# The transposes of the rotary queries behind the key projections instead of behind the query projections

## The chip, the core and the metric

The kernel runs on one of the eight cores of a Trainium2 chip. A core has a matrix engine (TensorE, PE in the profile; PEld is its loading of weights), a vector engine (VectorE, DVE), an activation engine (ScalarE, ACT), GpSimdE (POOL) and SyncE (SP), which here only issues DMAs. Matrix products go to PSUM, which has eight banks of 512 float32 columns per partition; VectorE and ScalarE read them from there into SBUF. The metric is the device time of one launch in microseconds.

## The reference

The reference is a trunk of two post-norm layers over 256 positions of width 2048, in float32. The first layer mixes positions with a gated MLP, the second with latent attention; each mixer is followed by a gated MLP with a causal convolution, and each of the four sub-layers ends in a layer norm of `ALPHA * x + sublayer(x)`. The change lies in the attention, which is, cut to what matters:

```python
def mla_mixer(x, w_in, q_norm_g, kv_norm_g, w_q_b, w_kv_b, w_out, cos, sin):
    h = x @ w_in                                  # 2048 -> 512 + 512 + 64
    c_q, c_kv, k_rope = split(h)
    q = (rms_norm(c_q) @ w_q_b)                   # 16 heads of 128 + 64
    q_nope, q_rope = split(q)
    q_rope, k_rope = apply_rope(q_rope), apply_rope(k_rope)
    kv = (rms_norm(c_kv) @ w_kv_b)                # 16 heads of 128 + 128
    k_nope, v = split(kv)
    s = (q_nope . k_nope + q_rope . k_rope) * SM_SCALE   # per head, masked by chunks of 64
    return softmax(s) @ v, then @ w_out
```

Each head's score is a sum of two products: one over 128 columns that are not rotated, one over 64 that are. The rotated key is shared by all heads.

## The kernel before

The kernel is one straight program; there is no loop on the chip. A layer above the instructions keeps the order in which the code issues them, engine by engine, and adds the waits. All weights come from HBM as tiles of 128 x 2048 float32 (1 MB), through one list in the order of use (`Feed`, lines 48 to 92). A tile of weights is loaded into `raw` (line 62, from SP's queue). ScalarE rounds it to a narrower format as `wh` (line 75), VectorE writes the rest `raw - wh` as `wl` (line 76), each in two halves of 1024 columns. A product is then the sum of three: high times high, low times high, high times low. `feed.next()` gives the next tile and issues the splits of the two after it and the loads of two more.

All large tiles share one pool of 22 slots of SBUF (`big`), so a load or a split may have to wait until the last reader of an earlier tile has left its slot. All PSUM tiles share the eight banks (`bank`, pool `ps`) in the same way: the first matmul into a new bank waits for the last reader of the tile that had the bank before.

The part around the change is straight-line code:

1. Rotary queries (lines 609 to 618): the product for the 64 rotated columns of all 16 heads into four banks `qr`, for two halves b of the positions and two halves f of the columns. Between its two chunks stand the transposes `ct` of the key latent and `krt` of the rotated key.
2. Rotation (lines 619 to 622): VectorE reads each of the four banks in four operations (lines 527 to 530) and finishes in two more (531, 532). The result, `qr` in SBUF, is rounded by ScalarE and its rest taken by VectorE into `qrs`, one tile for each half of the positions (lines 626, 627).
3. `qr_put(b, f)` (lines 630 to 635): four transposes of `qrs[b]` for heads 4f to 4f+3 into a bank `qrt`, and a ScalarE copy of the bank into `qrT`.
4. `heads` (lines 638 to 651): 48 matmuls into four banks for four heads; then, for each bank, a ScalarE copy (line 649) and a VectorE subtraction (line 650) that split the result into `qnT` or `knT`. It is called four times for the queries (`qn`, tiles qn0 to qn3) and four times for the keys (`kn`).
5. The values `vv` (lines 715 to 729), in two halves; the scores of the first two heads begin inside the second half (`attend_a`, line 663). `attend_a` reads `qnT`, `knT`, `qrT` and `krT`. Then come the other heads, four steps ahead of the output projection.

In the kernel before, two calls of `qr_put` stand behind each of the four query blocks: qn0 is followed by heads 0 to 7 of the first half of the positions, and so on.

Of the kernel before, what the change touches and what calls it, by code (L numbers as in the profile page):

```python
# [95 lines left out]
def trunk(ctx: ExitStack, tc: tile.TileContext, x, xT, gm_in, gm_wout, ffn_up, ffn_dn,  # L96
# [9 lines left out]
    def slot(shape, name, dt=F32):  # L106
        return big.tile(shape, dt, tag="big", name=name)

    def bank(name):
        return ps.tile([P, 512], F32, tag="bank", name=name)  # L110

    def mm(o, l, r, start, stop):
        nc.tensor.matmul(o, l, r, start=start, stop=stop, skip_group_check=True)  # L113
# [516 lines left out]
    def qr_put(b, f):  # L630
        t = bank(f"qrt{b}{f}")
        for j in range(4):
            nc.tensor.transpose(t[:, j * P : (j + 1) * P], qrs[b][:, 4 * f + j].rearrange("p n c -> p (n c)"), ident)
        h = 4 * (f % 2)
        nc.scalar.copy(qrT[f // 2][:, h : h + 4, b * P : (b + 1) * P], t.rearrange("p (j c) -> p j c", j=4))


    def heads(dst, src, i, tag):
        hi, lo = feed.next()
        acc = [bank(f"{tag}{i}_{f}") for f in range(4)]  # L640
        for k in range(4):
            t = src[0][:, k, :]
            for n, (x, w) in enumerate(((t[:, 0:S], hi), (t[:, S : 2 * S], hi), (t[:, 0:S], lo))):
                for f in range(4):
                    o = k * 512 + f * P
                    mm(acc[f][:, 0:S], w[:, o : o + P], x, k == 0 and n == 0, k == 3 and n == 2)
        t = slot([P, 4, 2 * S], f"{tag}T{i}", F32R)
        for f in range(4):
            nc.scalar.copy(t[:, f, 0:S], acc[f][:, 0:S])
            nc.vector.tensor_tensor(t[:, f, S : 2 * S], acc[f][:, 0:S], t[:, f, 0:S].bitcast(F32), ALU.subtract)  # L650
        dst.append(t)

    for i in range(4):
        heads(qT, cq, i, "qn")
        for j in range(2):
            qr_put(i // 2, 2 * (i % 2) + j)
    for i in range(4):
        heads(kT, ckv, i, "kn")

    oT = []  # L660
    probs = {}
# [207 lines left out]
```

## Time and profile before

| | |
|---|---|
| time, median of three runs | 2544.89 us (2543.96, 2544.89, 2544.93) |
| time of the profiled execution | 2543.96 us |
| its span, first to last instruction | 2542.2 us |
| TensorE busy | 2524.2 us (99%) |
| mean granted TensorE clock | 0.998 |
| VectorE busy, ScalarE busy | 1575.4 us, 1230.3 us |
| HBM read | 476.00 MB, 188 GB/s over the span |

The profile is one execution; its times are microseconds from the first instruction. A row of the view in order of time gives the start, the duration, the engine, the line, the operation with `out<-in` by the program's names without numbers, the shape and how many instructions were merged; in brackets stands the idle time of the engine before it and what ended it. A row of a view by stretches gives the busy time of each engine within the stretch and the clock that TensorE was granted, as a share of full speed. A row of the waits names who waited for whom, the total, the number of times and the longest. Ends of matmuls are modelled, so the starts are what the arguments go by.

### The profile page before, as it was taken

How to read it: one execution, taken by the hardware profiler on the slowest of the kernel's cores; microseconds unless marked ns; L12 is line 12 of the kernel's file. 1: busy time of each engine (PE TensorE's matmuls, PEld its weight loads, DVE VectorE, ACT ScalarE, POOL GpSimd, SP SyncE). 2: the span in 40 equal slices, each digit the busy share in tenths (PEclk: the TensorE clock that was granted, in tenths of full speed). 3: DMA queues.
4: the chain of work that ended last, by engine and by line, in shares of the span. 5: the costliest groups of instructions: out<-in, count | busy, mean ns of one | idle time of the engine just before them, and what ended most of it. 6: DMA issues, size and time to landing. Idle time of an engine off the chain costs nothing.

```text
span 2542.2 us, 32529 instructions
## 1 busy us (share of the span) xinstructions
PE 2524.2 (99%) x13203; PEld 2161.4 (85%) x13203; DVE 1575.4 (62%) x2286; ACT 1230.3 (48%) x1805; POOL 2.9 (0%) x17
## 2 busy tenths in 40 slices
PE   9999999999999999999999999999999999999998
PEld 7888888888888888888888888988888888888886
DVE  6444675675455767665775547656676576667554
ACT  6343444455443555554554443555365555546441
POOL 0000000000000000000000000000000000000000
PEclk9999999999999999999999999999999999999999
DMA  8445444456564545555565553334555455546552
GB/s 338 183 169 195 166 177 172 174 214 225 201 221 165 205 166 202 184 180 183 185 226 202 207 221 146 122 142 177 187 199 182 166 199 182 182 168 246 209 199 89
DMA packets 68838, 480.20 MB, mean 189 GB/s; under 512 B 7632, under 2 KB 8272, under 8 KB 11728
## 3 DMA queue, kind: packets, MB, share of 16 engines
q1 hardware_dynamic: 68688, 478.13, 51.5%
q8 instruction: 103, 1.69, 0.3%
q14 instruction: 47, 0.39, 0.0%
HBM read 476.00 MB, written 2.10 MB: 188 GB/s over the span
## 4 chain that ended last, share of the span: by engine, by line
PE 98%; DVE 1%; DMA 0%; ACT 0%; SPq 0%; issue 0%; DVEq 0%; ACTq 0%
PE up L113 36%; PE dn L113 18%; PE u L113 11%; PE wo L113 10%; PE v L113 10%; PE mo L113 3%; PE upf L113 2%; PE mkv L113 1%; PE kn L113 1%; PE mq L113 1%; PE vv L113 1%; PE s L113 1%; PE qn L113 1%; PE sc L113 1%; PE qr L113 0%; PE lnt L369 0%
## 5 line engine op out<-in xcount | busy, mean ns | idle before, releaser
L76 DVE TENSOR_TENSOR wl<-raw,wh 128x1024 fp32r<-128x1024 f32 (+2 forms) x886 | 1054.3, 1215 | 534.5 <-ACT wh L75 375.5
L75 ACT CAST wh<-raw 128x1024 fp32r<-128x1024 f32 (+2 forms) x886 | 891.4, 1045 | 558.1 <-DVE wl L76 219.3
L113 PE MATMUL up<-xhl,wh 128*128 128x512 f32 x2624 | 715.1, 393 | 0.0
L113 PEld LDWEIGHTS up<-xhl,wh 128*128 128x128 f32 x2624 | 447.8, 188 | 54.9
L113 PEld LDWEIGHTS up<-xhl,wl 128*128 128x128 f32 x2624 | 403.5, 188 | 59.4
L113 PE MATMUL up<-xhl,wl 128*128 128x256 f32 x2624 | 420.1, 281 | 0.0
L113 PE MATMUL wo<-wh,woa 128*128 128x512 f32 x768 | 236.8, 389 | 0.0
L113 PE MATMUL v<-wh,xhl 128*128 128x512 f32 x768 | 235.8, 391 | 0.2 <-ACT wh L75 0.2
L113 PE MATMUL u<-xhl,wh 128*128 128x512 f32 x768 | 217.3, 396 | 0.0
L113 PE MATMUL dn<-wh,dn0a 128*128 128x512 f32 x688 | 212.2, 389 | 0.0
L113 PE MATMUL dn<-wh,dn1a 128*128 128x512 f32 x688 | 211.9, 389 | 0.0
L113 PEld LDWEIGHTS v<-wh,xhl 128*128 128x128 f32 x768 | 144.6, 188 | 31.4 <-ACT wh L75 0.6
L113 PEld LDWEIGHTS wo<-wh,woa 128*128 128x128 f32 x768 | 144.0, 188 | 29.9
L113 PEld LDWEIGHTS dn<-wh,dn1a 128*128 128x128 f32 x688 | 129.1, 188 | 26.9
L113 PEld LDWEIGHTS dn<-wh,dn0a 128*128 128x128 f32 x688 | 129.0, 188 | 26.5
L113 PE MATMUL wo<-wl,woa 128*128 128x512 f32 x384 | 149.2, 389 | 0.0
L113 PEld LDWEIGHTS u<-xhl,wh 128*128 128x128 f32 x768 | 131.5, 189 | 19.2 <-issue 1.1
L113 PE MATMUL v<-wl,xhl 128*128 128x512 f32 x384 | 147.2, 389 | 0.0
L113 PEld LDWEIGHTS u<-xhl,wl 128*128 128x128 f32 x768 | 121.3, 189 | 15.9
L113 PE MATMUL dn<-wl,dn0a 128*128 128x512 f32 x344 | 133.8, 389 | 0.0
L113 PE MATMUL dn<-wl,dn1a 128*128 128x512 f32 x344 | 133.8, 389 | 0.0
L113 PE MATMUL u<-xhl,wl 128*128 128x256 f32 x768 | 130.8, 281 | 0.0
(208 smaller groups left out, 2119.3 us busy)
## 6 DMA issues: line engine op xcount, KB each, us to landing
raw<-in_ffn_up_dram SPq DMA_DIRECT2D x172, 1024.0 KB, 4.8
raw<-in_gm_in_dram SPq DMA_DIRECT2D x95, 1024.0 KB, 4.8
raw<-in_ffn_dn_dram SPq DMA_DIRECT2D x86, 1024.0 KB, 4.7
raw<-in_gm_wout_dram SPq DMA_DIRECT2D x48, 1024.0 KB, 4.8
raw<-in_ml_out_dram SPq DMA_DIRECT2D x16, 1024.0 KB, 4.8
raw<-in_ml_b_dram SPq DMA_DIRECT2D x14, 1024.0 KB, 4.8
raw<-in_ml_kv_dram SPq DMA_DIRECT2D x5, 864.0 KB, 4.6
lng<-in_ln_rows_dram SPq DMA_DIRECT2D x4, 1024.0 KB, 6.7
```

The lines of the kernel that those rows point to most:

```text
L75: self.nc.scalar.copy(hi[:, c], raw[:, c])
L76: self.nc.vector.tensor_tensor(lo[:, c], raw[:, c], hi[:, c].bitcast(F32), ALU.subtract)
L113: nc.tensor.matmul(o, l, r, start=start, stop=stop, skip_group_check=True)
```

## The change

The eight calls of `qr_put` move from the loop over the query blocks to the loop over the key blocks, two behind each. Their order changes too: behind block i come heads 4i to 4i+3 of both halves of the positions, where before all heads of the first half came first.

```diff
     for i in range(4):
         heads(qT, cq, i, "qn")
-        for j in range(2):
-            qr_put(i // 2, 2 * (i % 2) + j)
     for i in range(4):
         heads(kT, ckv, i, "kn")
+        for b in range(2):
+            qr_put(b, i)
```

On TensorE the 32 transposes, in four groups of eight, then stand behind kn0 to kn3. On ScalarE the eight copies of line 635 stand behind the copies of the same key blocks. VectorE's and SP's instructions keep their order; which slot and which bank each tile gets, and so what its first writer waits for, changes from qn1 on. `qrs` is held until the last key block.

## The prediction

> **What bounds the kernel now.** I read the page first, then TensorE's waits, then the region around the moved transposes in order of time, engine by engine.
>
> ```profile
> span 2542.2 us, 32529 instructions
> PE 2524.2 (99%) x13203; PEld 2161.4 (85%) x13203; DVE 1575.4 (62%) x2286; ACT 1230.3 (48%) x1805; POOL 2.9 (0%) x17
> PE 98%; DVE 1%; DMA 0%; ACT 0%; SPq 0%; issue 0%; DVEq 0%; ACTq 0%
> ```
>
> TensorE's waits (engine and line that waited, for whom: us in total, times, longest):
>
> ```profile
> PE qrt L633 <- DVE qrs L627: 3.2, 1, 3.2
> PE o L113 <- ACT pts L700: 2.4, 1, 2.4
> ```
>
> TensorE is busy for 99% of the span and is 98% of the chain that ended last. So an edit that keeps its instructions can win only where it stands still or runs slowly. The largest wait of the whole run is at the first transposes of the rotary queries (qrt, line 633): 3.2 us until VectorE has written qrs. The edit moves exactly these transposes. TensorE in order of time (start, duration, instructions, and in brackets the idle time before them):
>
> ```profile
> 1608.31 1.12 PE L113 MATMUL qn<-cq,wh 128*128 128x256 f32 x8
> ...
> 1609.75 1.12 PE L113 MATMUL qn<-cq,wh 128*128 128x256 f32 x8
> ...
> 1612.15 0.64 PE L113 MATMUL qn<-cq,wl 128*128 128x256 f32 x4
> 1615.97 1.97 PE L633 MATMUL qrt<-ident,qrs 128*128 128x128 f32 x8 [3.19 <-DVE qrs L627]
> ...
> 1625.38 1.03 PE L633 MATMUL qrt<-ident,qrs 128*128 128x128 f32 x8
> 1626.17 1.19 PE L113 MATMUL qn<-cq,wh 128*128 128x256 f32 x8
> ...
> 1632.00 1.04 PE L633 MATMUL qrt<-ident,qrs 128*128 128x128 f32 x8
> ```
>
> Twelve matmuls go from 1608.31 to 1609.75, so one slot is 0.12 us and the 48 of a block of four heads take 5.76. The undisturbed round of eight transposes and 48 matmuls runs from 1625.38 to 1632.00: 6.62. The first round is different. The last four matmuls of qn0 start at 1612.15, so the next slot was free at 1612.63. From there to the end of that round is 1625.38 - 1612.63 = 12.75. The round therefore costs 12.75 - 6.62 = 6.13 more than an undisturbed one. The wait explains 1615.97 - 1612.63 = 3.34 of it. The other 2.79 is slowness after the wait, as the granted clock shows (columns: stretch, its length, then the busy time of PE, PEld, DVE, ACT and POOL, the clock as a share of full speed, DMA share, GB/s):
>
> ```profile
> 1611.60:1615.00 3.40, 1.19 (x10) 0.98 (x9) 3.40 (x11) 0.40 (x2) 0.00 (x0) 1.00 0.00 0
> 1615.00:1618.40 3.40, 2.43 (x12) 2.43 (x13) 3.37 (x4) 3.40 (x6) 0.00 (x0) 0.50 0.00 0
> 1618.40:1621.80 3.40, 3.40 (x17) 3.31 (x17) 3.32 (x6) 3.37 (x6) 0.00 (x0) 0.50 0.37 82
> 1622.00:1622.50 0.50, 0.50 (x6) 0.50 (x5) 0.50 (x2) 0.00 (x0) 0.00 (x0) 1.00 1.12 475
> ...
> 1686.60:1690.10 3.50, 2.41 (x20) 2.05 (x18) 3.06 (x5) 1.03 (x3) 0.00 (x0) 1.00 0.54 166
> 1690.10:1693.50 3.40, 2.08 (x16) 1.99 (x17) 1.14 (x4) 2.77 (x8) 0.00 (x0) 1.00 0.36 142
> ```
>
> The clock fell to 0.50 during the wait and came back only near 1621.8, inside qn1. The other long wait, 2.4 us near 1690 (o on pts), kept the clock at 1.00. So what the edit can win here is the 6.13, half of it hidden in matmuls that only look busy.
>
> **The change part by part.** It removes nothing and adds nothing: 32 transposes and eight ScalarE copies (line 635) move from behind qn0 to qn3, eight and two each, to behind kn0 to kn3.
>
> *The wait goes.* Behind qn0 now comes qn1, which does not read qrs. Behind kn0, some 25 us later, qrs has long been written. That gives back 6.13. It is the whole sum unless something else is late for qn1 or qn2, so I look at what is late next.
>
> *First new wait, qn1.* Each block takes four of the eight PSUM banks. In the changed program qn1 takes those of ct and qr, the fourth of them from qr of rows b=1, columns f=1. That bank is free when the rotation of that piece has read it for the last time, in line 530. VectorE in order of time:
>
> ```profile
> 1613.70 0.41 DVE L530 TENSOR_TENSOR qr<-qr,rope_sb 128x256 f32<-128x256 f32 x1
> ...
> 1614.70 2.48 DVE L627 TENSOR_TENSOR qrs<-qr,qrs 128x1024 f32<-128x1024 f32 x2
> 1617.09 2.35 DVE L76 TENSOR_TENSOR wl<-raw,wh 128x1024 fp32r<-128x1024 f32 x2
> 1619.36 1.41 DVE L650 TENSOR_TENSOR qnT<-qn,qnT 128x256 fp32r<-128x256 f32 x4
> 1620.86 2.36 DVE L76 TENSOR_TENSOR wl<-raw,wh 128x1024 fp32r<-128x1024 f32 x2
> ```
>
> Nothing on VectorE ahead of 1614 depends on what TensorE does after qn0, so this time stays: 1613.70 + 0.41 = 1614.11. TensorE started 0.05 behind the first qrs (1614.70 + 1.22 = 1615.92, then 1615.97), so I add that: 1614.16. It would have reached the fourth matmul of qn1 at 1612.63 + 3 x 0.12 = 1612.99. Wait: 1.17. Queued behind it on TensorE is everything, so it counts in full.
>
> *Second new wait, qn2.* Its four banks are those of qn0, free when line 650 has subtracted from them. VectorE's row stays where it is, since it stands behind qrs and a weight split, neither of which moves: its fourth piece ends at 1619.36 + 1.41 = 1620.77, with the 0.05 at 1620.82. TensorE would be at the fourth matmul of qn2 at 1614.16 + 48 x 0.12 = 1619.92. Wait: 0.90. It can't be less unless VectorE gets there sooner. In the kernel before, both waits lie inside the 6.13.
>
> *Third block and on.* VectorE then splits weights to 1623.22 and drains qn1 in four pieces of some 0.35, to about 1624.6. TensorE needs those banks from 1620.82 + 45 x 0.12 = 1626.22: no wait, by 1.6. From there on all stands in the order that the undisturbed rounds show.
>
> *The transposes at their new place.* Behind kn0 they cost what they cost behind qn1: 6.62 a round against 5.76 a block, 0.86 each. Four rounds there, none in the query part. The price changes only if the new place has a wait. Their banks are freed by the drains of the block before, as in the rounds shown, and ScalarE has the room for two copies of 0.55 in each key block. Rows for ScalarE, and for VectorE in the rounds with transposes:
>
> ```profile
> 1618.78 1.10 ACT L635 CAST qrT<-qrt 128x512 fp32r<-128x512 f32 x2
> ...
> 1650.84 1.20 ACT L649 CAST knT<-kn 128x256 fp32r<-128x256 f32 x4 [2.67 <-PE kn L113]
> ...
> 1634.99 2.36 DVE L76 TENSOR_TENSOR wl<-raw,wh 128x1024 fp32r<-128x1024 f32 x2 [1.33 <-ACT wh L75]
> 1638.86 1.42 DVE L650 TENSOR_TENSOR qnT<-qn,qnT 128x256 fp32r<-128x256 f32 x4 [1.51 <-ACT qnT L649]
> ```
>
> ScalarE idles 2.67 before it drains a key block and gets 1.10 more work: hidden by 1.57. Were that cover gone, the 1.10 would push the drains, and TensorE with them, 1.10 a block, 4.4 in all. VectorE idles 1.51 even in a round with transposes. The copies finish about 1 us into vv; their first reader is the score of head 0, behind the first half of vv, and vv runs for some 24 us: cover over 10.
>
> ```profile
> L113 PEld LDWEIGHTS vv<-wh,ckv x64: 187/188/201, 1662.4 to 1686.2; 128*128 128x128 f32 x64
> ```
>
> *The slots and SP's queue.* qrs holds two of the 22 slots from which weights are loaded, and now until kn3. No DMA moves, but SP issues loads in order, and a load that waits for a slot holds all behind it.
>
> ```profile
> 1626.44 0.33 SPq L62 DMA_DIRECT2D raw<-in_ml_b_dram  x1
> ...
> 1662.71 0.33 SPq L62 DMA_DIRECT2D raw<-in_ml_out_dram  x1
> ...
> DMA to landing us min/median/max: 4.6/4.7/7.7
> ...
> 1674.36 2.01 ACT L75 CAST wh<-raw 128x1024 fp32r<-128x1024 f32 x2
> ```
>
> The load at 1626.44 waited for the second group of transposes; in the changed program it takes a slot freed by a weight split before 1620. The slots of qrs go to later loads instead, the last to the first ml_out weights, now issued at 1662.71 behind kn3. That one will wait for the last transposes, 0.86 behind kn3. It lands 4.7 later, 1667.4, and is split at 1674.36: 7.0 of slack, 6.1 after. Taken at 0; bounds: 0, and 9.8 if the slack were gone (one load 4.7, a split of 1.05 on ScalarE and 1.22 on VectorE, and 2.79 for a clock that falls).
>
> *Sum.* -6.13 + 1.17 + 0.90 = -4.06, rounded to -4.0 since the fourth matmul starts a little behind its weight load. The profiled execution took 2543.96 and is the fastest of three; it would become 2540.0. The median is 2544.89, 0.93 above it: 2540.9, or 0.16% less. About 0.2%, 5.1 us, is what a measurement of this kernel can tell from no change, so I forecast a real gain that stays inside it.
>
> **The rivals.**
>
> *A, as summed:* 2540.9; its own range is 2540.0 to 2541.8, from the spread of 0.97 between the three runs.
>
> *B, the slow clock comes back elsewhere.* The fall from 1.00 came behind a stretch of 3.4 us in which TensorE was busy 1.19; stretches with 2.41 and 2.08 kept 1.00, whether they lie so by luck or not. The wait near 1690 moves 4 us earlier, and if a stretch of 3.4 us falls on it whole, TensorE is busy for 1.0 of it. Or the two waits in qn1 and qn2, 2.07 together, do it. Against the latter: they stand 5.6 us apart, each leaves at least 2.2 busy of 3.4. Price 2.79: 2543.7. The Trainium skill (TensorE: Matmul & The Clock Gate, "A second HAM failure mode: psum-queue depth-cycling") says that short idles between groups of matmuls, where PSUM banks are cycled, can make the clock swing, and so speaks against this change. No row here shows it for idles of about 1 us, and 2.41 us of idle did not do it in this trace.
>
> *C, the two bank waits do not bind:* banks come free earlier than I place them, so all 6.13 is won: 2538.8. Against: the VectorE rows are a queue without gaps there.
>
> *D, slower: the two slots.* With qrs held through the key part, the weights of the output projection come late and TensorE waits once: -4.0 + 9.8 = +5.8: 2550.7. It decides from the point at which that slot comes free more than 6.1 behind today's issue. For it: SP's queue is short of slots all through here; against: the slack above.
>
> *E, the wait only changes its name:* qn1 waits as long for its own bank, or its weights, as the transposes did for qrs, and the clock falls as before: 2544.9. Against: line 530 ends 1.8 before qrs.
>
> **How the numbers follow.** A 0.68, B 0.13, C 0.09, D 0.05, E 0.05. The likeliest gives 2540.9. The range runs from C's 2538.8 to B's 2543.8 and leaves out D and E. Faster by over 0.2% means under 2539.8: C, and 0.04 of A's edge, 0.13. Slower by over 0.2%: D, 0.05. Within: 0.82.
>
> **What would show it.** Right: no wait of qrt on qrs; a wait of qn on VectorE near 1613 of about 1.2, and a second near 1620 of about 0.9 in all; clock 1.00 throughout 1612 to 1622; key blocks 6.6 apart instead of 5.8; vv starting at about 1658.5 instead of 1662.5; from there the same distances as before. Wrong: a clock below 1.00 anywhere behind 1600, a wait of mo or sc on a weight split (the slots), a qrt that waits for a bank, or a longer first key block.

## The result and the profile after

The changed kernel takes 2540.57 us (median of 20 runs, 2539.30 to 2542.43) against 2544.64 for the kernel before in the same session (20 runs, 2542.84 to 2548.10). The medians are 4.07 us apart, 0.16%. The ratio of the means is 0.9981, since six of the 20 runs of the kernel before lie above 2547, and its interval is 0.9975 to 0.9988. So the gain is real, and the interval reaches from 0.12% to 0.25%. Forecast were 2540.9 and 4.0 us.

TensorE's waits in the changed kernel (engine and line that waited, for whom: us in total, times, longest):

```profile
PE o L113 <- ACT pts L700: 2.4, 1, 2.4
...
PE qn L113 <- DVE qnT L650: 1.3, 1, 1.3
```

The wait of qrt on qrs is gone. A wait of qn on the drain of a block (line 650) has come, 1.3 us. TensorE around it in order of time:

```profile
1612.53 0.64 PE L113 MATMUL qn<-cq,wl 128*128 128x256 f32 x4
1613.01 0.88 PE L113 MATMUL qn<-cq,wh 128*128 128x256 f32 x6
1613.73 0.52 PE L113 MATMUL qn<-cq,wl 128*128 128x256 f32 x3
...
1618.29 0.64 PE L113 MATMUL qn<-cq,wl 128*128 128x256 f32 x4
1620.23 0.51 PE L113 MATMUL qn<-cq,wh 128*128 128x256 f32 x2 [1.30 <-DVE qnT L650]
...
1637.61 1.04 PE L633 MATMUL qrt<-ident,qrs 128*128 128x128 f32 x8
1638.40 1.19 PE L113 MATMUL kn<-ckv,wh 128*128 128x256 f32 x8
...
1657.47 1.04 PE L633 MATMUL qrt<-ident,qrs 128*128 128x128 f32 x8
1658.26 0.70 PE L113 MATMUL vv<-wh,ckv 128*128 128x512 f32 x2
```

qn1 starts at 1613.01, right behind qn0, in groups of 6 and 3 where qn0 has 8 and 4. By these counts the matmuls of one bank stand behind the first ones of the other three. So the layer above the instructions does not always keep the order of the code, as it was said to do where the kernel before was described. The profile before shows it too. There qn1 begins in groups of 4 and 2:

```profile
1617.60 1.20 PE L113 MATMUL qn<-cq,wh 128*128 128x256 f32 x4
1618.60 0.63 PE L113 MATMUL qn<-cq,wl 128*128 128x256 f32 x2
```

The first of the two forecast waits does not show in the changed kernel. The second does. The slot behind the four matmuls at 1618.29 was free at 1618.77, and qn2 starts at 1620.23: 1.46 lost. The transposes at their new place take 0.79 before the next block starts, as before, and a key round lasts (1657.47 - 1637.61) / 3 = 6.62, as forecast. ScalarE and VectorE in the key blocks:

```profile
1638.52 1.12 ACT L635 CAST qrT<-qrt 128x512 fp32r<-128x512 f32 x2
...
1644.07 1.20 ACT L649 CAST knT<-kn 128x256 fp32r<-128x256 f32 x4 [2.55 <-PE kn L113]
...
1644.48 1.42 DVE L650 TENSOR_TENSOR knT<-kn,knT 128x256 fp32r<-128x256 f32 x4 [1.51 <-ACT knT L649]
```

ScalarE still idles 2.55 before it drains a key block, where the prediction left 1.57 of the 2.67: the transposes make the round longer as well. VectorE idles the forecast 1.51. The profiled execution took 2542.30, longer than 18 of the 20. Its clock by stretches (stretch, length, busy time of PE, PEld, DVE, ACT and POOL, clock, DMA share, GB/s) shows why:

```profile
1615.00:1618.40 3.40, 3.40 (x30) 3.40 (x30) 3.36 (x4) 3.13 (x5) 0.00 (x0) 1.00 0.29 55
1618.40:1621.80 3.40, 2.10 (x18) 1.90 (x17) 3.40 (x7) 3.40 (x9) 0.00 (x0) 1.00 0.90 296
...
1683.70:1687.10 3.40, 1.14 (x11) 0.86 (x9) 2.29 (x7) 1.19 (x6) 0.00 (x0) 1.00 0.74 287
1687.10:1690.50 3.40, 3.25 (x13) 3.07 (x14) 0.94 (x3) 2.04 (x5) 0.00 (x0) 0.51 0.06 24
1690.50:1693.90 3.40, 3.40 (x16) 3.13 (x16) 2.02 (x4) 1.08 (x2) 0.00 (x0) 0.50 0.65 219
```

The clock holds at 1.00 where it had fallen before, and falls at the next long wait instead, that of the first product of probabilities and values (o). That is rival B, in this execution.

The stage from the first weight load of qn0 to that of vv is the yardstick for what follows. It reads from two rows of one tile each, here of the changed kernel: 1658.2 - 1607.1 = 51.1, against 1662.4 - 1606.7 = 55.7 before (the second of these two rows stands in the prediction, the first is the last one below). The part without any loss would be 8 blocks of 5.76 and 4 x 0.86 for the transposes: 49.5.

```profile
L113 PEld LDWEIGHTS qn<-cq,wh x128: 186/192/192, 1607.1 to 1631.1; 128*128 128x128 f32 x128
L113 PEld LDWEIGHTS vv<-wh,ckv x64: 187/188/201, 1658.2 to 1682.1; 128*128 128x128 f32 x64
```

```profile
L113 PEld LDWEIGHTS qn<-cq,wh x128: 187/192/338, 1606.7 to 1637.9; 128*128 128x128 f32 x128
```

What comes behind the stage, from the first weight load of vv to the end of the span, is called the rest below: 2540.5 - 1658.2 = 882.3 in the changed kernel, 2542.2 - 1662.4 = 879.8 before.

### The profile page after: what moved, and what is told of

Read it like the earlier page. It is cut to its first block, busy times and chain, and to the rows that moved or that the text cites. A ratio compares the mean times of both kernels' runs of the same rounds, so it can differ in the third digit from the quotient of the medians.

```text
span 2540.5 us, 32528 instructions
## 1 busy us (share of the span) xinstructions
PE 2523.8 (99%) x13203; PEld 2160.7 (85%) x13203; DVE 1575.1 (62%) x2286; ACT 1233.3 (49%) x1805; POOL 2.9 (0%) x17
## 4 chain that ended last, share of the span: by engine, by line
PE 98%; DVE 1%; DMA 0%; ACT 0%; SPq 0%; issue 0%; DVEq 0%; ACTq 0%
PE up L113 36%; PE dn L113 18%; PE u L113 11%; PE wo L113 10%; PE v L113 10%; PE mo L113 3%; PE upf L113 2%; PE mkv L113 1%; PE kn L113 1%; PE mq L113 1%; PE vv L113 1%; PE s L113 1%; PE sc L113 1%; PE o L113 0%; PE qn L113 0%; PE qr L113 0%
## 5 line engine op out<-in xcount | busy, mean ns | idle before, releaser
L113 PEld LDWEIGHTS up<-xhl,wh 128*128 128x128 f32 x2624 | 447.8, 188 | 54.8
```

## The experiments

Eight kernels were run. The median of the kernel before differs a little between sessions: 2544.41 (33 runs) beside one block later, wait filled, drain first and two more slots held; 2544.31 (28 runs) beside the other four. So the table gives the distance to the median of the same session as well.

| kernel | median, us | under before, us | from | to | runs | stage, us | rest, us |
|---|---|---|---|---|---|---|---|
| before (first session) | 2544.64 | | 2542.84 | 2548.10 | 20 | 55.7 | 879.8 |
| changed | 2540.57 | 4.07 | 2539.30 | 2542.43 | 20 | 51.1 | 882.3 |
| one block later | 2540.63 | 3.78 | 2539.67 | 2542.24 | 11 | 51.1 | 881.0 |
| wait filled | 2542.66 | 1.75 | 2541.39 | 2544.11 | 11 | 53.1 | 882.2 |
| drain first | 2539.15 | 5.26 | 2538.09 | 2540.59 | 11 | 49.6 | 881.1 |
| two more slots held | 2541.34 | 3.07 | 2539.86 | 2542.92 | 11 | 51.6 | 880.0 |
| changed, wait of o filled | 2539.64 | 4.67 | 2539.21 | 2540.18 | 11 | 51.1 | 879.8 |
| before, wait of o filled | 2543.35 | 0.96 | 2542.87 | 2545.21 | 11 | 54.8 | 879.7 |
| wait half filled | 2542.76 | 1.55 | 2541.14 | 2543.62 | 11 | 53.1 | 879.8 |
| drain first, head 0 early | 2536.45 | 7.86 | 2536.26 | 2536.61 | 6 | 49.6 | 877.9 |

The stage and the rest are from one profiled execution each. The rest of the first nine rows falls into three groups. It is 879.7 to 880.0 in the five profiles whose clock stayed at 1.00 there, 881.0 and 881.1 in the two where it was at 0.50 for 3.4 us behind the wait of o, and 882.2 and 882.3 in the two where it was for 6.8 us. So a fall of the clock at that wait costs about 1.2 or 2.4 us. Far ahead of the stage, in the first 500 us, TensorE waits 0.2 to 1.8 us in all for the inputs of a tile v, and that differs from profile to profile as well; it is in the medians and not in these two columns.

### The transposes one block later, in the query part

```diff
     for i in range(4):
         heads(qT, cq, i, "qn")
-        for j in range(2):
-            qr_put(i // 2, 2 * (i % 2) + j)
+        if i > 0:
+            for j in range(2):
+                qr_put((i - 1) // 2, 2 * ((i - 1) % 2) + j)
     for i in range(4):
         heads(kT, ckv, i, "kn")
+        if i == 0:
+            for j in range(2):
+                qr_put(1, 2 + j)
```

> The kernel before, with each pair of transposes one block later, still in the order of heads of the kernel before: behind qn1, qn2, qn3 and kn0. Theory (what is won is that qn1 does not stand behind qrs; the place in the key part is worth nothing): no wait of qrt on qrs, clock 1.00 near 1615 to 1622, a wait of qn2 on the drain of qn0 of about 1.3 us as in the changed kernel, time within 1 us of the changed kernel's (2540.6), 4 us under before. Rival (the key part is the better place, because ScalarE and the weight splits have more room there): the time lies between the two, at 2542 to 2545.

2540.63, 3.78 under before where the changed kernel is 4.07 under, and the same stage time. The wait stands at the same place, now under the name of the transposes behind qn1, which want the same banks as qn2 would:

```profile
PE o L113 <- ACT pts L704: 2.4, 1, 2.4
...
PE qrt L633 <- DVE qnT L650: 1.3, 1, 1.3
```

So the key part as a place is worth nothing that these runs resolve; the two distances are 0.3 apart. What counts is that one block of work stands between qn0 and the transposes.

### The wait filled with work that nobody reads

```diff
     for i in range(4):
         heads(qT, cq, i, "qn")
+        if i == 0:
+            fill = bank("fill")
+            for _ in range(15):
+                mm(fill, idle[:, 0:P], idle, True, True)
         for j in range(2):
             qr_put(i // 2, 2 * (i % 2) + j)
```

> The kernel before, with 15 matmuls of 128x512 bf16 into a spare bank between qn0 and the first transposes, whose result nobody reads: they fill the wait of 3.3 us, and the transposes start when qrs is ready, as before. Theory (2.8 us of the loss is the slow clock behind the wait): clock 1.00 from 1612 to 1622, the first round of transposes and qn1 takes about 6.6 us instead of 9.4 from the first transpose, time 2.5 to 3 us under before (2544.6), about 2541.9. Rival (the wait of 3.3 us is the whole loss, the slow clock only shows in the records or is made up behind it): same time as before, within 0.7 us.

The 3.3 us stay lost here; only the clock is helped. TensorE in order of time, and the clock by stretches:

```profile
1612.93 3.41 PE L113 MATMUL fill<-idle 128*128 128x512 bf16 x14
1616.28 1.09 PE L633 MATMUL qrt<-ident,qrs 128*128 128x128 f32 x8
...
1623.12 1.04 PE L633 MATMUL qrt<-ident,qrs 128*128 128x128 f32 x8
```

```profile
1612.60:1616.00 3.40, 3.35 (x19) 1.67 (x18) 3.40 (x9) 0.83 (x1) 0.00 (x0) 1.00 0.00 0
1616.00:1619.40 3.40, 3.40 (x29) 3.13 (x28) 3.37 (x4) 3.40 (x8) 0.00 (x0) 1.00 0.00 0
```

The round of transposes and qn1 takes 1623.12 - 1616.28 = 6.84 instead of 9.41: 2.57 of real time, not of records alone. The stage is 53.1, 2.6 under before. The median fell by 1.75 only, less than the 2.5 to 3 expected: in the profiled execution (2544.11) the clock fell in the wait of o. The quickest executions, 2541.39 and 2541.44, are half a microsecond under where the theory put the median. The interval of the ratio, 0.9985 to 1.0002, does not leave out the same time; but seven of the 11 runs are under 2542.89, the fastest of the 33 before.

### Half of the filling work

The same with 7 matmuls.

> The kernel before with 7 instead of 15 filling matmuls between qn0 and the first transposes: an idle time of about 1.8 us is left of the 3.3. Theory (an idle time of that length leaves the clock alone more often than not): time as with 15, about 2542.7, clock 1.00 near 1615 to 1622. Rival (any idle time over 1.5 us lets it fall): 2544 or more, and a clock of 0.50 for 3.4 or 6.8 us there.

An idle time of 1.7 is left, and the clock stays at 1.00 in the profiled execution (2541.14), though TensorE is busy for only half of the stretch:

```profile
PE qrt L633 <- DVE qrs L627: 1.7, 1, 1.7
```

```profile
1612.60:1616.00 3.40, 1.69 (x8) 0.76 (x8) 3.37 (x8) 1.37 (x2) 0.00 (x0) 1.00 0.00 0
1616.00:1619.40 3.40, 3.40 (x30) 3.32 (x29) 3.40 (x4) 3.40 (x8) 0.00 (x0) 1.00 0.00 0
```

With 2542.76 the median is that of 15 matmuls, and again seven of the 11 runs are under the fastest before, 2542.83. Idle times of 1.3 to 1.7 us did not cost clock in any profile taken here, so the wait that the change leaves in qn2 costs only itself there.

### The drain of qn0 ahead of qrs

```diff
     qrs = []
-    for b in range(2):
-        t = slot([P, H, 2, ROPE], f"qrs{b}")
-        ...
     for i in range(4):
         heads(qT, cq, i, "qn")
+        if i == 0:
+            for b in range(2):
+                t = slot([P, H, 2, ROPE], f"qrs{b}")
+                ...
```

> The changed kernel, with the rounding of the rotary queries into qrs issued behind the block qn0 instead of ahead of it, so that the split of the next weights and the drain of qn0 come first on ScalarE and VectorE. Theory (the remaining wait in qn2 is the drain of qn0, queued behind qrs): that wait goes, the query part runs without a gap, about 1.4 us under the changed kernel (2540.6), 2539.2. Rival (another bank or a weight is late by then, 1 us or more): no gain, the wait of qn2 or qn3 stands on a weight split or on qn1's drain.

2539.15: 5.26 under before, 1.19 more than the changed kernel, and 1.48 under one block later, which ran beside it. VectorE drains qn0 at 1617.02 instead of 1619.76, and TensorE goes through qn2 without a gap:

```profile
1614.75 2.35 DVE L76 TENSOR_TENSOR wl<-raw,wh 128x1024 fp32r<-128x1024 f32 x2
1617.02 1.41 DVE L645 TENSOR_TENSOR qnT<-qn,qnT 128x256 fp32r<-128x256 f32 x4
1618.35 2.35 DVE L654 TENSOR_TENSOR qrs<-qr,qrs 128x1024 f32<-128x1024 f32 x2
```

```profile
1617.96 0.64 PE L113 MATMUL qn<-cq,wl 128*128 128x256 f32 x4
1618.44 0.40 PE L113 MATMUL qn<-cq,wh 128*128 128x256 f32 x2
```

The stage is 49.6, against 49.5 for the part without any loss: next to nothing is left to win in it by order alone.

### Two more slots held

```diff
+    held = [slot([P, D], f"held{i}") for i in range(2)]
+    for t in held:
+        nc.gpsimd.memset(t[:, 0:1], 0.0)
     for i in range(4):
         heads(qT, cq, i, "qn")
     ...
+    for i in range(2):
+        mm(bank(f"rel{i}")[:, 0:1], qrs[i][:, 0].rearrange("p n c -> p (n c)"), held[i][:, 0:1], True, True)
```

> The changed kernel, with two more of the 22 slots held from ahead of qn0 until two added one-column matmuls behind kn3 read them: twice the number of slots that the change itself holds longer. Theory (the weight loads have slack, the slots that qrs keeps cost nothing): loads are issued later, no wait of TensorE on a weight split near 1600 to 1700, time within 0.7 us of the changed kernel. Rival (the slots are at their edge): TensorE waits for a split in the key or value part, and the time rises by 2 us or more.

2541.34 is 0.71 over one block later, which ran beside it, and 0.77 over the changed kernel: at the edge of the 0.7 expected, and far from the rival's 2. The stage is 0.5 longer (51.6), at the added matmuls, and the wait of o is 2.7 instead of 2.4; together that is about the difference. No wait on a weight split came up in the key and value parts, though SP's queue now does wait for slots that the added matmuls give back (they read both the held slots and those of qrs):

```profile
SPq L62 <- PE rel L113: 8.9, 1, 8.9
```

```profile
PE o L113 <- ACT pts L705: 2.7, 1, 2.7
...
PE qn L113 <- DVE qnT L650: 1.3, 1, 1.3
```

The loads have slack for two slots more than the change takes. Rival D is out.

### The wait of o filled, in both kernels

```diff
+        if t == 2:
+            fill = bank("fill")
+            for _ in range(11):
+                mm(fill, idle[:, 0:P], idle, True, True)
         if 0 <= t - 2 < H:
             attend_c(t - 2)
```

> The changed kernel, with 11 matmuls of 128x512 bf16 into a spare bank ahead of the first product of probabilities and values, whose result nobody reads: they fill the wait of 2.4 us near 1687, which stays as long. Theory (in most executions of the changed kernel the clock falls in that wait, for 3.4 or 6.8 us, and costs about 1.3 or 3 us): clock 1.00 throughout 1600 to 1790, all executions close to the fastest ones of the changed kernel, median about 2539.4, 1 us under it, spread under 2 us. Rival (the spread has another cause, the start of the program or the DMAs, and the slow clock there is hidden by ScalarE and VectorE): median and spread as the changed kernel's, 2540.6 and 3 us.

> The kernel before with the same 11 matmuls at the same place. Theory (there the clock falls at the transposes in every execution, and in the wait near 1690 as well only in a part of them, the executions at 2546.5 to 2548): that group goes, the others stay, median about 2544.0. Then the change's own gain, with the second wait made harmless in both kernels, is 2544.0 - 2539.4 = 4.6 us. Rival (the group has another cause): it stays, one run in five above 2546.5.

The changed kernel comes to 4.67 under before, 0.60 more than without (0.93 if the medians are compared as they are), and its spread falls from 3.13 to 0.97; the clock holds throughout 1600 to 1790 in the profiled execution. So the slow clock behind the wait of o is real in this kernel and takes 0.6 to 0.9 us of the median. That fits the 1.2 or 2.4 us that a fall costs, in a part of the executions. In the kernel before, none of the 11 runs is above 2546, where 6 of 28 beside it are; with that share 11 runs without one come about once in 14 by chance, so this is likely, not certain. Its median fell to 2543.35 and its runs lie in two groups, six from 2542.87 to 2543.35 and five from 2544.06 to 2545.21. The profiled execution (2543.06) is of the lower one, and there the slow clock behind the transposes lasts 3.4 us, not the 6.8 of the profile before:

```profile
1612.80:1616.20 3.40, 0.21 (x3) 0.21 (x3) 3.37 (x9) 1.31 (x2) 0.00 (x0) 1.00 0.00 0
1616.20:1619.60 3.40, 3.40 (x17) 3.15 (x15) 3.40 (x4) 3.40 (x8) 0.00 (x0) 0.50 0.00 0
1619.60:1621.00 1.40, 1.40 (x12) 1.40 (x13) 1.32 (x5) 1.40 (x3) 0.00 (x0) 0.99 0.52 76
```

Its stage is 54.8 against 55.7. With the wait of o made harmless in both kernels the change is worth 2543.35 - 2539.64 = 3.7 by the medians, under the 4.6 expected, which took the long fall for every execution. This median lies at the upper edge of the lower group; with one run more in the upper one it would be 2544.06, and the change worth 4.4. So 3.7 to 4.4 is what these runs tell. The stages say the same: 54.8 - 51.1 = 3.7 for the short fall, 55.7 - 51.1 = 4.6 for the long one.

### A version that beats both

Drain first, and the transposes of head 0's probabilities inside the second half of vv:

```diff
                     prod_b(acc[b], x_parts(ckv, k, b), ...)
+                if hf == 1 and k == 2:
+                    attend_b(0)
...
-            attend_b(t - 1) if t - 1 != 1 else (attend_b(0), attend_b(1))
+            attend_b(t - 1)
```

> The changed kernel with the drain of qn0 ahead of the rounding into qrs, and with the transposes of head 0's probabilities moved ahead into the second half of the value product, so that their copy on ScalarE stands ahead of the four copies of vv. Theory (the wait near 1687 is head 0's probabilities queued on ScalarE behind vv, and both waits cost what they show): the wait of o shrinks from 2.4 to under 1 us and the clock holds, time 1 to 3 us under the drain-first kernel (2539.15), 2536 to 2538. Rival (head 1's probabilities are then waited for as long): as the drain-first kernel, 2539.

2536.45, the ratio to before 0.9968 (0.9956 to 0.9980), and six runs within 0.35 us. The wait of o is gone; 1.0 us of waiting for head 2's probabilities is left:

```profile
PE pt L699 <- DVE p L691: 1.0, 1, 1.0
```

The reason given for the wait was not the one that bound. In the changed kernel the copy of head 0's probabilities (line 700) stood behind the four copies of vv and also behind head 2's exponential (line 686). The copies of vv had ended at 1683.54. Behind them ScalarE idled 2.38 for VectorE, until it could start that exponential, and the copy came last. Moving the copy ahead took it out of both queues:

```profile
1681.13 2.41 ACT L729 COPY vv<-vv 128x512 f32<-128x512 f32 x4
1685.91 0.37 ACT L686 ACTIVATE p<-sc,mx 128x128 f32<-128x128 f32 x1 [2.38 <-DVE mx L684]
...
1686.72 0.86 ACT L700 COPY pts<-pt 128x384 f32<-128x384 f32 x2
```

## Why the prediction was right

*The loss at the first transposes, 6.13.* Right in kind. That the wait and the slow clock are two separate losses is shown: filling the wait alone gave back 2.57 of the 2.79 in its round. The size was one execution's. The clock falls for 3.4 or 6.8 us, and in the shorter case the stage loses 0.9 less.

*First new wait, 1.17.* Did not come. The bank is free when the step said: line 530 ends at 1614.51 in the changed kernel, where everything stands 0.4 later. But the step took qn1's matmuls in the order of the code. They stand in another order, with those of one bank behind, and from the counts these begin near 1616.0, when line 530 is long over.

```profile
1614.09 0.42 DVE L530 TENSOR_TENSOR qr<-qr,rope_sb 128x256 f32<-128x256 f32 x1
```

*Second new wait, 0.90.* Came, with 1.46: qn2 waits from its first bank on, since qn1 had lost no time. What it waits for is what the step named, VectorE's drain of qn0 behind qrs, and the drain-first run shows that this was the only loss left: 1.2 to 1.5 us back, and a stage of 49.6. The two terms together were 2.07 forecast and 1.46 measured.

*Transposes in the key part at no extra cost.* Right: rounds of 6.62, with ScalarE idle 2.55 and VectorE 1.51 in them. The slots at 0: right, by two more slots held.

*The sum.* By the two profiles the stage gained 55.7 - 51.1 = 4.6, over the 4.06 of the sum by the 0.6 of the two waits. The medians gained 4.07. That this agrees so closely is luck. The sum took the long fall of the clock from one profile, and with the short one the stage gains 3.7. It left out the slow clock behind the wait of o, which falls in a part of the executions of both kernels; with that wait filled the change is worth 3.7 to 4.4. How much of the 4.07 comes from there is not resolved.

*Rivals.* B was given 0.13 as an all-or-nothing case at 2543.7. A clock below 1.00 behind 1600 was also one of the signs that the prediction named for being wrong, and it came in the profile. But B happens in a part of the executions, at the wait of o and not at the bank waits, and a fall there costs about 1.2 or 2.4 us and not 2.79: a term of the median of both kernels that should have stood in the sum. The Trainium skill's rule on cycling PSUM banks (TensorE: Matmul & The Clock Gate, "A second HAM failure mode: psum-queue depth-cycling") is about short idle times that come back with every group of matmuls. No run here tests that: the waits of 1.3 us at a bank and 1.7 us at qrs are single ones, and left the clock at 1.00 in every profile that has them. C had neither wait binding: the first did not, by the order of the matmuls and not by an earlier bank, and the second did. D fell with the held slots. E fell with the waits of the changed kernel.

## What to carry to other kernels

Where TensorE bounds a kernel, read the granted clock behind each long wait as well as the wait: here 3.2 us of waiting hid up to 2.8 us more in matmuls that count as busy. To remove a wait, put one block of independent work ahead of the waiting instruction. Here it mattered little how much further back the instruction went, but the queue that then drained the banks of the block before did matter. Take the order of the matmuls from the trace and not from the code. And where a loss depends on a clock that falls in some executions, forecast the median from several, not from the one that was profiled.

## What the runs showed of the hardware

The clock changed on a grid of time. In each of the ten profiles the changes lie whole multiples of 3.413 us apart. In the kernel before it rose at 7.34, fell at 1615.01, which is 471 of them later, and rose again at 1621.84, two later. So it can be asked what TensorE did in each stretch of 3.41 us on that grid.

Behind every stretch in which TensorE was busy 1.43 us or less, the clock fell to 0.50; behind every one with 1.52 or more it stayed at 1.00. This holds for all ten profiles from the first rise to the fall at the end of the program; ends of matmuls are modelled, so the two limits are only as good as that. The six falls behind a wait came after 0.22, 1.00, 1.00, 1.12, 1.19 and 1.43. The last of these is that of the wait-filled run, at the wait of o:

```profile
1685.32:1688.73 3.41, 1.43 (x13) 1.15 (x11) 2.37 (x5) 1.03 (x6) 0.00 (x0) 1.00 0.86 286
1688.73:1692.14 3.41, 2.98 (x12) 2.81 (x13) 1.14 (x4) 2.05 (x6) 0.00 (x0) 0.50 0.07 26
```

With two more slots held the same wait is longer, 2.7 us, but an edge of the grid divides it, and the clock held:

```profile
1683.10:1686.51 3.41, 1.79 (x16) 1.51 (x15) 2.74 (x5) 0.75 (x2) 0.00 (x0) 1.00 0.68 245
1686.51:1689.92 3.41, 2.34 (x18) 2.25 (x19) 1.17 (x5) 2.78 (x9) 0.00 (x0) 1.00 0.16 65
```

An idle time of 2.41 us can thus let it fall or not, by where it lies: the wait of o is that long in the profiles of both kernels, held the clock in the one before (2.31 and 2.10 busy) and lost it in the changed one (1.12). An idle time of 1.7 us leaves 1.7 of a stretch that is busy otherwise, over both limits, wherever it lies; that is an estimate from these figures.

How long the clock stays down goes by the first slow stretch. Where TensorE was busy for all of it, the clock came back behind it: one block later (below), drain first, and before with the wait of o filled. Where the wait ran on into it, with 2.45 busy in the kernel before, 2.98 with the wait filled and 3.30 in the changed kernel, a second slow one followed. That one was busy throughout, and then the clock came back. Six falls are few, but all six fit.

```profile
1683.94:1687.35 3.41, 1.00 (x7) 0.72 (x6) 2.13 (x7) 1.67 (x6) 0.00 (x0) 1.00 0.66 262
1687.35:1690.76 3.41, 3.41 (x17) 3.31 (x16) 1.40 (x2) 2.26 (x3) 0.00 (x0) 0.50 0.17 29
1690.76:1692.00 1.24, 1.24 (x12) 1.19 (x11) 0.78 (x3) 0.37 (x1) 0.00 (x0) 1.00 0.73 198
```
